# Parameters in the rows of the first input tile, first weights in pieces of two steps, first loads held in order

## The chip, the cores and the metric

The kernel runs on one core of one Trainium2 chip. The metric is the device time of one execution in microseconds; a kernel's time is the median of several runs.

## The reference

The reference is a decoder trunk of two layers on one sequence of 1024 tokens with 1024 features, in float32. Each layer is

```
h = rmsnorm(x, attn_norm);  proj = h @ w_in            # split among four mixers
y = latent attention | gated convolution | causal pooling | sliding-window attention
x = x + (rmsnorm of each group(y) * mix_norm) @ w_o
gate, up = split(rmsnorm(x, ffn_norm) @ w_gate_up);  x = x + (silu(gate) * up) @ w_down
```

and a last rmsnorm follows the layers. The part that matters here is the very first one: the norm of x, and the products of x with the columns of `w_in` that give the keys, the values and the queries of the sliding-window attention.

## The kernel before

Everything is held transposed: features on the 128 partitions, tokens along the rows. The 1024 features are eight *steps* k of 128, the 1024 tokens two *halves* t of 512, so x is sixteen tiles x(t,k) of 128 x 512. A float32 product is made of three products of a faster type: each operand is split into a high half (a rounded copy by ScalarE, L363 or, with a gain, L368) and a low half (the remainder, by VectorE, L366 or L369), and `mm3` (L343) adds high x high, high x low and low x high in PSUM. Each x(t,k) is multiplied by its gain `attn_norm`, a column of the tile `par` that holds all norm weights of the program. The factor 1/rms comes after the product: the squares of x are summed tile by tile (L398, L407, L415, L409), and TensorE adds over the partitions with a matrix of ones (L426).

The opening of layer 0 stands in the order L559 to L617. TensorE runs `WARM` products of ones with ones (L562), while the first loads arrive. The weights of keys and values (`wkv`) are loaded each in two halves of four steps (`first_half`, L472) and split (`first_split`); the tiles of x come through `enter_load` (L458), the parameters in a load of their own (L565), the raw weights of the first queries at L573. Then for each half of the tokens and each step, `enter` splits x(t,k), the key and the value product take it (`first_terms`), and `enter_sum` adds its squares. The query products (`proj`) follow.

SBUF is cut into 47 places of 128 x 1024 numbers (`Slots`), taken as pairs or as halves; a load into a half that was used before must wait until its readers are done. The order of instructions is not the written one: `scheduled_kernel` traces the program, `Order` plans a start for every instruction of each engine from a table of costs and its due times, tries small random shifts (`improve`), and imposes the order found on all engines, SyncE's loads among them. `behind(a, b)` adds a rule without a wait to this: a must stand behind b on its engine. Buffers and PSUM banks are given out from the planned ends too, so an edit at the start can move instructions anywhere.

Of the kernel before, what the change touches and what calls it, by code (L numbers as in the profile page):

```python
# [14 lines left out]
F32 = mybir.dt.float32  # L15
# [5 lines left out]
P = 128  # L21
D = 1024
S = 1024
L = 2
HT = 512
NK = D // P
# [15 lines left out]

NSP = 3
NG = NFF // 2
WARM = 12
DN_SUMS = tuple(range(4, 20))
DN_MADE = ()

# [2 lines left out]
PC_N = 39  # L51
# [74 lines left out]
def trunk_kernel(ctx: ExitStack, tc: tile.TileContext, ins, out, given=None, ends=None):  # L126
# [11 lines left out]
    R, F = View(slots, F32R), View(slots, F32)  # L138
# [2 lines left out]
        return ap.bitcast(F32)  # L141


    par = cpool.tile([P, L * PC_N + NK], F32, name="par")
    cst = cpool.tile([P, CC_N], F32, name="cst")
    ident = cst[:, CC_ID : CC_ID + P]
    ones = cpool.tile([P, P], F32, name="ones")
# [189 lines left out]
    def mm3(o, terms, start=True, stop=True, again=False):  # L337

        nonlocal last_mm
        n = len(terms)  # L340
        for k, (wh, wl, rh, rl) in enumerate(terms):
            for i, (w, r) in enumerate(((wh, rh), (wh, rl), (wl, rh))):
                last_mm = pe.matmul(  # L343
                    o,
                    w,
                    r,
                    start=start and k == 0 and i == 0,
                    stop=stop and k == n - 1 and i == 2,
                    skip_group_check=again,
                )  # L350
# [10 lines left out]
    def split(hi, lo, f, gain=None, after=None):  # L361
        if gain is None:
            a = act.copy(hi, f)  # L363
            if after is not None:
                behind(a, after)
            dve.tensor_tensor(out=lo, in0=f, in1=rd(hi), op=ALU.subtract)  # L366
        else:
            a = act.activation(hi, f, AF.Copy, scale=gain)  # L368
            dve.scalar_tensor_tensor(  # L369
                out=lo, in0=f, scalar=gain, in1=rd(hi), op0=ALU.mult, op1=ALU.subtract  # L370
            )
        return a
# [82 lines left out]

    def enter_load(t, k):
        s = xf[k][t] = F.half()
        sp.dma_start(F.ap(s), x_in[k, :, t * HT : (t + 1) * HT])  # L458

    def enter(t, k):  # L460
        if xf[k][t] is None:
            enter_load(t, k)
        hh[k][t] = half_split(F.ap(xf[k][t]), pcol(0, PC_ATTN + k))
# [2 lines left out]
        ss.add(t, F.ap(xf[k][t]))  # L466
        F.free(xf[k][t])

    def first_half(w, i):

        s = F.half()
        sp.dma_start(F.ap(s), w[2][:, i * HT : (i + 1) * HT])  # L472
        w[3].append(s)

    def first_split(w, i):

        cs = slice(i * HT, (i + 1) * HT)
        split(R.ap2(w[0])[:, cs], R.ap2(w[1])[:, cs], F.ap(w[3][i]))
        F.free(w[3][i])

    def first_terms(w, t, k):
        hi, lo = (R.ap2(i)[:, k * P : (k + 1) * P] for i in w[:2])
        return [(hi, lo, R.ap(hh[k][t][0]), R.ap(hh[k][t][1]))]

    def finish(x, t, cols):
# [15 lines left out]
    for l in range(L):  # L501
# [57 lines left out]
        if l == 0:  # L559
            warm = ps("pv")  # L560
            for i in range(WARM):
                pe.matmul(warm[:, :P], ones, ones, start=True, stop=True)  # L562
            wkv = [(R.pair(), R.pair(), ins["w_in"][0, m], []) for m in (2, 3)]
            enter_load(0, 0)
            sp.dma_start(par, ins["params"])  # L565
            for i in range(2):
                for w in wkv:
                    first_half(w, i)
                for k in range(4 * i, 4 * i + 4):
                    if k:  # L570
                        enter_load(0, k)
            raw = F.pair()
            sp.dma_start(F.ap2(raw), ins["w_in"][0, 0])  # L573
            for k in range(NK):
                enter_load(1, k)
            sp.dma_start(cst, ins["const"])
            pkv = []
            for t in range(2):
                pkv.append([ps("mm"), ps("s")])
                for k in range(NK):  # L580
                    if t == 0 and k % 4 == 0:
                        for w in wkv:
                            first_split(w, k // 4)
                    enter(t, k)
                    for p, w in zip(pkv[t], wkv):
                        mm3(p, first_terms(w, t, k), k == 0, k == NK - 1)
                    enter_sum(t, k)
                if t == 0:
                    wq0 = tuple(R.ap2(i) for i in ring_next())
                    split(*wq0, F.ap2(raw))  # L590
                    F.free_pair(raw)
                    pq = [proj(wq0, 0, "s")]
                ratt[t] = ss.rnorm(t)
            dve.tensor_copy(e_r, cst[:, CC_E : CC_E + P])
            for i in range(L):
                for o, c, n in ((nsink, PC_SINK, 4), (nffn, PC_FFN, NK)):
                    dve.tensor_scalar(
                        out=o[:, i * n : i * n + n],
                        in0=par[:, i * PC_N + c : i * PC_N + c + n],
                        scalar1=-1.0,  # L600
                        scalar2=None,
                        op0=ALU.mult,
                    )
            for v in wkv:
                R.free_pair(v[0])
                R.free_pair(v[1])
            pk, pv_ = zip(*pkv)
            pq.append(proj(wq0, 1, "t"))
        else:
            wk = take()  # L610
            pk = [proj(wk, 0, "s")]
            wv = take()
            pv_ = [proj(wv, 0, "s")]
            pk.append(proj(wk, 1))
            pv_.append(proj(wv, 1, "s"))
            w = take()
            pq = [proj(w, 0, "s"), proj(w, 1, "t")]  # L617
# [1632 lines left out]
def _layout(i):  # L2250
    def tiles(w):

        l, k, n = w.shape
        return w.reshape(l, k // P, P, n // P, P).transpose(0, 3, 2, 1, 4)

    def cols(v):

        return v.reshape(L, -1, P).transpose(2, 0, 1)

    c = np.ascontiguousarray  # L2260
    a = {}
    a["xT"] = c(i["x"].reshape(S, D).T).reshape(NK, P, S)
    w = i["w_in"]
    o = np.cumsum([0, 256, 128, 32, 256, 256, 256, 256, 256, 128, 128])
    cq, ckv, kr, gb, gc, u, pl, q, k, v = (w[:, :, o[n] : o[n + 1]] for n in range(10))
    a["w_in"] = c(
        tiles(
            np.concatenate(
                [q, k, v]
                + [t[:, :, s : s + P] for s in (0, P) for t in (u, gc, gb)]  # L2270
                + [cq, ckv, pl],
                axis=2,
            )
        )
    ).reshape(L, 15, P, D)
    kr = np.concatenate([kr, kr[:, :, 16:], kr[:, :, :16]], axis=2)
    a["w_kr"] = c(kr.reshape(L, NK, P, 64).transpose(0, 2, 1, 3)).reshape(L, P, HT)
    uq = i["w_uq"].reshape(L, 2, P, HEADS, 96)
    uq = np.concatenate([uq, uq[..., 80:], uq[..., 64:80]], axis=4)
    a["w_uq"] = c(uq.transpose(0, 2, 3, 1, 4)).reshape(L, P, 1024)  # L2280
    ukv = i["w_ukv"].reshape(L, P, HEADS, 2, 64)
    a["w_ukv"] = c(ukv.transpose(0, 1, 3, 2, 4)).reshape(L, P, 512)
    a["w_o"] = c(tiles(i["w_o"])).reshape(L, NK, P, D)

    gu = tiles(i["w_gate_up"]).reshape(L, 2, NFF, P, NK // 2, 2, P).transpose(0, 1, 2, 3, 5, 4, 6)

    a["w_gu"] = c(
        np.stack(
            [
                np.stack([gu[:, 0, :, :, 0], gu[:, 1, :, :, 1]], axis=3),  # L2290
                np.stack([gu[:, 0, :, :, 1], gu[:, 1, :, :, 0]], axis=3),
            ],
            axis=2,
        )
    ).reshape(L, NFF, 2, P, D)
    dn = tiles(i["w_down"]).reshape(L, NK // 2, 2, P, NG, 2, P)

    a["w_dn"] = c(dn.transpose(0, 1, 2, 5, 3, 4, 6)).reshape(L, NK // 2, 4, P, NG * P)
    pw = np.zeros((L, P, 2, 2, 64), i["pool_w"].dtype)
    for ct in range(2):  # L2300
        for g in range(2):
            pw[:, 64 * g : 64 * g + 64, ct, g] = i["pool_w"][:, 2 * ct + g]
    a["pool_w"] = c(pw.reshape(L, P, 256))
    conv = i["conv_w"].reshape(L, 3, 2, P).transpose(3, 0, 1, 2).reshape(P, L, 6)
    sinks = np.broadcast_to(i["swa_sinks"][None], (P, L, 4))
    lay = np.concatenate(
        [
            cols(i["attn_norm"]),
            cols(i["ffn_norm"]),
            cols(i["mix_norm"]),  # L2310
            cols(i["mla_q_norm"]),
            cols(i["mla_kv_norm"]),
            conv,
            cols(i["pool_scale"]),
            sinks,
        ],
        axis=2,
    )
    fin = i["final_norm"].reshape(NK, P).T
    a["params"] = c(np.concatenate([lay.reshape(P, -1), fin], axis=1))  # L2320
    a["rope_q"], a["rope_k"], a["const"] = _constants()
    return a

# [27 lines left out]
```

## Time and profile before

| | |
|---|---|
| median of 3 runs | 2038.76 us (2038.35 to 2038.97) |
| the profiled execution | 2038.94 us, of it span 2037.2 us |
| busy TensorE | 2023.3 us (99%) |
| busy VectorE, ScalarE, GpSimd | 1543.7 us (76%), 1015.1 us (50%), 564.1 us (28%) |
| granted TensorE clock | 0.999 |

The span runs from the first instruction to the last; 1.7 us of the execution's time lie around it. Engines are PE (TensorE), DVE (VectorE), ACT (ScalarE), POOL (GpSimd) and SP (SyncE, which issues the loads). A row of the timeline has the start, the duration, the engine, the line of the kernel, the operation and what it writes and reads; behind `[` stands how long the engine was idle before and what ended that. Matmuls overlap, so the pitch from one to the next is what counts, not the duration of one.

### The profile page before, as it was taken

The numbers are of one execution on the slowest core, as the hardware profiler recorded it, in microseconds if no ns is written. First come the engines' busy times: TensorE is split into PE (matmuls) and PEld (weight loads), VectorE is DVE, ScalarE is ACT, GpSimd is POOL, SyncE is SP. The second block draws the span as 40 slices with busy tenths as digits, with TensorE's granted clock in tenths as the row PEclk, the third lists the DMA queues.
The fourth block names the chain that finished last, engine by engine and source line by source line (L and its number), as shares of the span: only waits on it lengthen the run. The fifth ranks groups of instructions, "written<-read, shape, count | busy, mean of one in ns | idle before, by whom it ended". The sixth has DMA issues, their size and how long they took to land.

```text
span 2037.2 us, 26750 instructions
## 1 busy us (share of the span) xinstructions
PE 2023.3 (99%) x9422; PEld 1677.9 (82%) x9422; DVE 1543.7 (76%) x2449; ACT 1015.1 (50%) x1766; POOL 564.1 (28%) x428
## 2 busy tenths in 40 slices
PE   9999999999999999999999999999999999999998
PEld 7887888878888888888888878888888888888887
DVE  8779979997677778767646898889966766775555
ACT  7447657753333335555533676677433333354342
POOL 0100000047776783000001000000677777710000
PEclk9999999999999999999999999999999999999999
DMA  5531222434555556999835223242454555487552
GB/s 206 106 66 47 72 97 82 155 124 166 187 178 188 177 173 238 367 344 325 283 118 122 63 93 120 92 144 96 146 194 170 194 175 169 160 293 266 182 185 84
DMA packets 154231, 338.56 MB, mean 166 GB/s; under 512 B 15088, under 2 KB 62192, under 8 KB 154096
## 3 DMA queue, kind: packets, MB, share of 16 engines
q1 hardware_dynamic: 149616, 325.31, 46.3%
q0 software_dynamic: 4480, 11.54, 3.2%
q8 instruction: 74, 1.21, 0.2%
q14 instruction: 61, 0.50, 0.1%
HBM read 241.36 MB, written 105.91 MB: 170 GB/s over the span
## 4 chain that ended last, share of the span: by engine, by line
PE 97%; DVE 1%; issue 1%; ACT 0%; DMA 0%; POOL 0%; SPq 0%; DVEq 0%; ACTq 0%; POOLq 0%
PE ps_mm L343 38%; PE ps_s L343 29%; PE ps_t L343 12%; PE ps_pv L343 8%; PE ps_pv L1111 2%; PE ps_t L1099 1%; PE ps_s L1045 1%; PE ps_s L1047 1%; PE ps_s L1046 1%; PE ps_s L659 1%; PE ps_s L917 1%; PE ps_pv L720 1%; PE ps_t L708 1%; PE ps_t L423 0%; DVE u L366 0%
## 5 line engine op out<-in xcount | busy, mean ns | idle before, releaser
L343 PE MATMUL ps_mm<-u,u 128*128 128x512 f32 (+1 forms) x3378 | 831.9, 389 | 2.1 <-ACT u L368 0.7
L343 PEld LDWEIGHTS ps_mm<-u,u 128*128 128x128 f32 x3378 | 616.1, 188 | 125.4 <-issue 2.4
L343 PE MATMUL ps_s<-u,u 128*128 128x512 f32 x2670 | 636.4, 390 | 0.7 <-ACT u L1339 0.5
L366 DVE TENSOR_TENSOR u<-u,u 128x1024 fp32r<-128x1024 f32 (+3 forms) x429 | 493.8, 1174 | 187.4 <-ACT u L363 131.1
L363 ACT CAST u<-u 128x1024 fp32r<-128x1024 f32 (+3 forms) x429 | 370.6, 883 | 443.4 <-PE ps_mm L343 62.8
L343 PEld LDWEIGHTS ps_s<-u,u 128*128 128x128 f32 x2670 | 500.9, 188 | 107.0 <-ACT u L1339 1.3
L343 PE MATMUL ps_t<-u,u 128*128 128x512 f32 (+1 forms) x1124 | 256.3, 378 | 0.1
L343 PEld LDWEIGHTS ps_t<-u,u 128*128 128x128 f32 x1124 | 202.5, 188 | 40.8 <-DVE u L1515 1.5
L1523 POOL TENSOR_TENSOR tp<-tp,u 128x512 f32<-128x512 f32 x80 | 125.0, 1562 | 352.3 <-ACT tp L1521 215.9
L343 PE MATMUL ps_pv<-u,u 128*128 128x512 f32 x744 | 177.1, 389 | 0.0
L343 PEld LDWEIGHTS ps_pv<-u,u 128*128 128x128 f32 x744 | 139.7, 188 | 29.0
L317 POOL DMA_DIRECT2D gd<-in_w_gu x24 | 21.4, 894 | 415.8 <-PE ps_t L343 282.0
L1108 POOL MEMSET u<- 128x128 f32 x32 | 6.3, 223 | 427.4 <-PE ps_pv L1111 117.6
L1521 ACT ACTIVATE tp<-tp 128x512 f32<-128x512 f32 x80 | 50.6, 633 | 129.3 <-DVE tp L442 129.2
L363 ACT CAST u<-ps_t 128x512 fp32r<-128x512 f32 (+3 forms) x132 | 64.7, 503 | 55.4 <-PE ps_t L1099 29.1
L366 DVE TENSOR_TENSOR u<-ps_t,u 128x512 fp32r<-128x512 f32 (+3 forms) x132 | 74.7, 580 | 13.3 <-ACT u L363 12.4
L368 ACT ACTIVATE u<-u,par 128x512 fp32r<-128x512 f32 x100 | 70.2, 717 | 29.2 <-DVE u L442 9.1
L1601 POOL TENSOR_TENSOR u<-u 128x352 f32<-128x352 f32 x64 | 77.0, 1204 | 8.6 <-DMA u<-in_w_dn 8.1
L369 DVE SCALAR_TENSOR_TENSOR u<-u,par,u 128x512 fp32r<-128x512 f32 x100 | 73.2, 746 | 6.3 <-ACT u L368 6.2
L1311 POOL TENSOR_TENSOR u<-u 128x512 f32<-128x512 f32 x38 | 69.9, 1840 | 27.2 <-DVE u L366 25.3
L1601 POOL TENSOR_TENSOR u<-u,u 128x352 f32<-128x352 f32 x64 | 76.4, 1194 | 2.7
L442 DVE TENSOR_TENSOR tp<-tp,u 128x512 f32<-128x512 f32 x76 | 75.3, 990 | 2.0
(204 smaller groups left out, 2314.0 us busy)
## 6 DMA issues: line engine op xcount, KB each, us to landing
u<-in_w_gu SPq DMA_DIRECT2D x84, 512.0 KB, 4.0
ad<-u SPq DMA_DIRECT2D x154, 256.0 KB, 2.4
u<-ad SPq DMA_DIRECT2D x70, 512.0 KB, 5.8
u<-in_w_dn SPq DMA_DIRECT2D x64, 352.0 KB, 3.4
qd<-u SPq DMA_DIRECT2D x64, 352.0 KB, 3.5
u<-in_w_in SPq DMA_DIRECT2D x43, 512.0 KB, 5.3
u<-qd SPq DMA_DIRECT2D x32, 512.0 KB, 5.5
u<-in_w_dn SPq DMA_DIRECT2D x24, 512.0 KB, 5.4
```

The source lines that it names most:

```text
L317: paced(pool.dma_start(d, a, **more))
L343: last_mm = pe.matmul(o, w, r, start=start and k == 0 and i == 0, stop=stop and k == n - 1 and i == 2, skip_group_check=again,)
L363: a = act.copy(hi, f)
L366: dve.tensor_tensor(out=lo, in0=f, in1=rd(hi), op=ALU.subtract)
L368: a = act.activation(hi, f, AF.Copy, scale=gain)
L369: dve.scalar_tensor_tensor(out=lo, in0=f, scalar=gain, in1=rd(hi), op0=ALU.mult, op1=ALU.subtract)
L442: dve.tensor_tensor(out=o, in0=a, in1=b, op=ALU.mult)
L1111: pe.matmul(py[:, c0:], v_of(j, h), R.ap(s)[:, c0:], start=j == 0 and n == 0, stop=j == nj - 1 and n == 1,)
L1311: pool.tensor_tensor(out=q4, in0=q4, in1=F.ap(self.raw[1] + 1), op=ALU.add)
L1521: last_silu = act.activation(g, g, AF.Silu)
L1523: pool.tensor_tensor(out=g, in0=g, in1=r, op=ALU.mult)
L1601: pool.tensor_tensor(out=o, in0=a, in1=b, op=ALU.add)
```

## The change

The parameters have no load of their own any more: they stand behind the numbers of x(0,0) in the rows of one array, `first`, of 128 x 598, which lands in a pair of halves; the gain of x(0,0) is read there, VectorE copies the parameters from the pair's second half to `par`, and this half becomes free. The first weights come in four pieces of two steps each, a piece of 512 columns holding both products (`w_first`). The loads of pieces and of the first half's tiles are tied to each other in the written order by `behind`. The warm-up has ten products in place of twelve.

```diff
-WARM = 12
+WARM = 10
...
     def enter_load(t, k):
         s = xf[k][t] = F.half()
-        sp.dma_start(F.ap(s), x_in[k, :, t * HT : (t + 1) * HT])
+        return sp.dma_start(F.ap(s), x_in[k, :, t * HT : (t + 1) * HT])
+
+    def enter_first():
+        s = F.pair()
+        loads.append(sp.dma_start(F.ap2(s)[:, : HT + PC_ALL], ins["first"]))
+        xf[0][0] = s
+        got = F.ap(s + 1)[:, :PC_ALL]
+        hh[0][0] = half_split(F.ap(s), got[:, PC_ATTN : PC_ATTN + 1])
+        dve.tensor_copy(par, got)
+        F.free(s + 1)
...
-    def first_half(w, i):
-        s = F.half()
-        sp.dma_start(F.ap(s), w[2][:, i * HT : (i + 1) * HT])
-        w[3].append(s)
-    def first_split(w, i):
-        cs = slice(i * HT, (i + 1) * HT)
-        split(R.ap2(w[0])[:, cs], R.ap2(w[1])[:, cs], F.ap(w[3][i]))
-        F.free(w[3][i])
-    def first_terms(w, t, k):
-        hi, lo = (R.ap2(i)[:, k * P : (k + 1) * P] for i in w[:2])
+    def first_terms(i, t, k):
+        cs = slice(2 * i * P + k % 2 * P, 2 * i * P + k % 2 * P + P)
+        hi, lo = (R.ap(v)[:, cs] for v in wkv[k // 2])
         return [(hi, lo, R.ap(hh[k][t][0]), R.ap(hh[k][t][1]))]
...
-            wkv = [(R.pair(), R.pair(), ins["w_in"][0, m], []) for m in (2, 3)]
-            enter_load(0, 0)
-            sp.dma_start(par, ins["params"])
-            for i in range(2):
-                for w in wkv:
-                    first_half(w, i)
-                for k in range(4 * i, 4 * i + 4):
-                    if k:
-                        enter_load(0, k)
+            wkv, wraw, loads = [], [], []
+            for j in range(NK // 2):
+                wraw.append(F.half())
+                loads.append(sp.dma_start(F.ap(wraw[j]), ins["w_first"][j]))
+                if j == 0:
+                    wkv.append(half_split(F.ap(wraw[0])))
+                    F.free(wraw[0])
+                    enter_first()
+                else:
+                    loads.append(enter_load(0, 2 * j))
+                loads.append(enter_load(0, 2 * j + 1))
+            for a, b in zip(loads[1:], loads):
+                behind(a, b)
             raw = F.pair()
             sp.dma_start(F.ap2(raw), ins["w_in"][0, 0])
...
-                    if t == 0 and k % 4 == 0:
-                        for w in wkv:
-                            first_split(w, k // 4)
-                    enter(t, k)
-                    for p, w in zip(pkv[t], wkv):
-                        mm3(p, first_terms(w, t, k), k == 0, k == NK - 1)
+                    if t == 0 and k and k % 2 == 0:
+                        wkv.append(half_split(F.ap(wraw[k // 2])))
+                        F.free(wraw[k // 2])
+                    if t or k:
+                        enter(t, k)
+                    for i, p in enumerate(pkv[t]):
+                        mm3(p, first_terms(i, t, k), k == 0, k == NK - 1)
```

SyncE's first loads before: `u4` to `u9` hold pieces of the weights of keys and values (L472) and the tiles x(0,0) to x(0,7) (L458), `par` the parameters, `u10` the raw query weights, `u11` and what follows the tiles of the second half.

```order
L472 DMA u4_120<-in_w_in 128x512
L458 DMA u4_120<-in_xT 128x512
L565 DMA par_75<-in_params 128x86
L472 DMA u5_124<-in_w_in 128x512
L458 DMA u5_124<-in_xT 128x512
L458 DMA u6_127<-in_xT 128x512 x2
L472 DMA u7_130<-in_w_in 128x512
L458 DMA u8_133<-in_xT 128x512
L472 DMA u7_130<-in_w_in 128x512
L458 DMA u8_133<-in_xT 128x512
L458 DMA u9_136<-in_xT 128x512 x2
L573 DMA u10_139<-in_w_in 128x1024
```

SyncE's first loads of the changed kernel: `u0` is the first piece of weights, `u2` the new first transfer; `u9` the raw query weights; the eight loads to `u8`, `u10`, `u11`, `u12` and `u13` are the tiles x(1,k) of the second half; the next load to `u2` is x(0,1), and `u4` takes the second piece of weights.

```order
L567 DMA u0_114<-in_w_first 128x512
L465 DMA u2_119<-in_first 128x598
L578 DMA u9_140<-in_w_in 128x1024
L459 DMA u8_138<-in_xT 128x512
L459 DMA u10_143<-in_xT 128x512
L459 DMA u11_146<-in_xT 128x512
L459 DMA u12_149<-in_xT 128x512
L459 DMA u13_152<-in_xT 128x512
L459 DMA u10_143<-in_xT 128x512
L459 DMA u11_146<-in_xT 128x512
L459 DMA u12_149<-in_xT 128x512
L459 DMA u2_119<-in_xT 128x512
```

x(0,1), which stood fifth, now stands twelfth, behind the query weights and all of the second half.

TensorE before, from the second real product on: `u15` is x(0,0), `u16` x(0,1), `u17` x(0,2), high and low half each; `u0` to `u3` are the weights of keys (`ps_mm`) and values (`ps_s`).

```order
L343 MATMUL ps_s_155<-u15_160,u2_118 128x512 x2
L343 MATMUL ps_mm_154<-u16_170,u0_116 128x512
L343 MATMUL ps_s_155<-u15_160,u3_119 128x512
L343 MATMUL ps_s_155<-u16_170,u2_118 128x512
L343 MATMUL ps_mm_154<-u16_170,u0_116 128x512
L343 MATMUL ps_mm_154<-u16_170,u1_117 128x512
L343 MATMUL ps_s_155<-u16_170,u2_118 128x512
L343 MATMUL ps_s_155<-u16_170,u3_119 128x512
L343 MATMUL ps_mm_154<-u17_182,u0_116 128x512
```

TensorE of the changed kernel, from the last product of x(0,0) with the first piece `u1` on: `u3` is x(0,0), `u24` and `u25` the high and low half of the query weights (`ps_s_261`), `u26` is x(1,0), `u27` x(1,1) and `u14` x(0,1); `ps_mm_295` and `ps_s_296` are the keys and values of the second half.

```order
L344 MATMUL ps_mm_155<-u3_121,u1_116 128x512
L344 MATMUL ps_s_261<-u3_121,u24_257 128x512 x2
L344 MATMUL ps_mm_295<-u26_297,u1_116 128x512
L344 MATMUL ps_s_296<-u26_297,u1_116 128x512
L344 MATMUL ps_s_261<-u3_121,u25_258 128x512
L344 MATMUL ps_mm_295<-u26_297,u1_116 128x512
L344 MATMUL ps_s_296<-u26_297,u1_116 128x512 x2
L344 MATMUL ps_s_296<-u27_307,u1_116 128x512 x3
L344 MATMUL ps_mm_295<-u26_297,u1_116 128x512
L344 MATMUL ps_mm_295<-u27_307,u1_116 128x512 x3
L344 MATMUL ps_s_156<-u14_164,u1_116 128x512
```

After x(0,0), TensorE now takes 3 products of the queries and 12 of the second half with the steps 0 and 1, and only then x(0,1).

More of the change, by code (lines that the diff above doesn't have):

```diff
@@ L141, in rd @@
         return ap.bitcast(F32)
-    par = cpool.tile([P, L * PC_N + NK], F32, name="par")
+    PC_ALL = L * PC_N + NK
+    par = cpool.tile([P, PC_ALL], F32, name="par")
     cst = cpool.tile([P, CC_N], F32, name="cst")
@@ L604, in trunk_kernel @@
             for v in wkv:
-                R.free_pair(v[0])
-                R.free_pair(v[1])
+                R.free(v[0])
+                R.free(v[1])
             pk, pv_ = zip(*pkv)
@@ L2319, in _layout @@
     fin = i["final_norm"].reshape(NK, P).T
-    a["params"] = c(np.concatenate([lay.reshape(P, -1), fin], axis=1))
+    a["first"] = c(np.concatenate([a["xT"][0, :, :HT], lay.reshape(P, -1), fin], axis=1))
+    two = a["w_in"][0, 2:4].reshape(2, P, NK // 2, 2 * P)
+    a["w_first"] = c(two.transpose(2, 1, 0, 3)).reshape(NK // 2, P, HT)
     a["rope_q"], a["rope_k"], a["const"] = _constants()
```

## The prediction

> **What bounds the kernel now.** I read the page's busy shares and chain first, then the stretches of the whole program, then the first 43 us in the timeline and the chain of waits.
>
> ```profile
> span 2037.2 us, 26750 instructions
> PE 2023.3 (99%) x9422; PEld 1677.9 (82%) x9422; DVE 1543.7 (76%) x2449; ACT 1015.1 (50%) x1766; POOL 564.1 (28%) x428
> PE 97%; DVE 1%; issue 1%; ACT 0%; DMA 0%; POOL 0%; SPq 0%; DVEq 0%; ACTq 0%; POOLq 0%
> ```
>
> TensorE ends almost everything: 97% of the chain is its own work. So a change can only move the time by moving TensorE's idle time, and the stretches show where that lies.
>
> ```profile
> core 0: us, PE busy (x) PEld busy (x) DVE busy (x) ACT busy (x) POOL busy (x), PEclk, DMA share, GB/s
> 0.00:42.60 42.60, 41.33 (x174) 32.99 (x175) 35.81 (x58) 34.48 (x56) 0.20 (x4) 1.00 0.60 216
> 42.60:430.00 387.40, 385.66 (x1890) 318.12 (x1888) 339.15 (x749) 241.96 (x522) 19.86 (x31) 1.00 0.31 89
> 430.00:1000.00 570.00, 569.95 (x2512) 471.08 (x2511) 420.98 (x438) 249.41 (x329) 260.85 (x181) 1.00 0.67 235
> 1000.00:1350.00 350.00, 349.07 (x1742) 291.26 (x1742) 263.37 (x640) 201.84 (x455) 13.84 (x28) 1.00 0.37 109
> 1350.00:2000.00 650.00, 649.73 (x2892) 537.85 (x2891) 464.73 (x526) 281.90 (x394) 269.37 (x184) 1.00 0.53 182
> ```
>
> From 42.6 to 2000 us TensorE is idle 1.74 + 0.05 + 0.93 + 0.27 = 2.99 us, out of 1957. The change rewrites the stretch before 42.6 us, where the first keys, values and queries are made:
>
> ```profile
> 0.75 0.39 SPq L472 DMA_DIRECT2D u<-in_w_in  x1
> 1.06 5.49 PE L562 MATMUL ps_pv<-ones 128*128 128x128 f32 x24 [1.06 <-DVE ones L148]
> 1.20 0.42 SPq L458 DMA_DIRECT2D u<-in_xT  x1
> 1.67 0.42 SPq L565 DMA_DIRECT2D par<-in_params  x1
> 3.49 0.62 ACT L363 CAST u<-u 128x512 fp32r<-128x512 f32 x1 [1.47 <-DMA u<-in_w_in]
> 5.94 0.72 ACT L368 ACTIVATE u<-u,par 128x512 fp32r<-128x512 f32 x1 [1.83 <-DMA par<-in_params]
> 6.71 1.52 PE L343 MATMUL ps_mm<-u,u 128*128 128x512 f32 x3 [0.16 <-ACT u L368]
> ```
>
> The warm-up products (12, each shown as two rows) end at 1.06 + 5.49 = 6.55; ScalarE gets the parameters only at 5.9, and the first real product starts at 6.71. The chain says what that costs:
>
> ```profile
> 1.67 4.18 DMA par<-in_params
> 20.58 0.86 PE ps_t L426 x2
> 35.98 0.93 PE ps_t L426 x2
> 37.15 5.46 PE ps_t L343 x24
> ```
>
> One real product takes 5.46 / 24 = 0.2275 us. The opening has 144 of them (keys and values 2 x 2 x 24, queries 2 x 24) and two norm sums of 0.86 and 0.93: 144 x 0.2275 + 1.79 = 34.55 us of work. It ends at 37.15 + 5.46 = 42.61, that is 36.06 after the warm-up: 1.5 us are lost to waits.
>
> **The change, part by part.** *Warm-up.* Two products fewer are four rows of 5.49 / 24 = 0.229 us: the warm-up ends at 1.06 + 20 x 0.229 = 5.64, which is 0.92 earlier. Nothing hides this, if data are there.
>
> *Parameters.* Their own load is gone, and with it ScalarE's 1.83 us of waiting. What is late next comes from the order of loads, whose rate these rows give:
>
> ```profile
> u<-in_w_in SPq DMA_DIRECT2D x1, 256.0 KB, 2.7
> u<-in_xT SPq DMA_DIRECT2D x1, 256.0 KB, 2.9
> par<-in_params SPq DMA_DIRECT2D x1, 43.0 KB, 4.2
> u<-in_w_in SPq DMA_DIRECT2D x1, 256.0 KB, 4.8
> 2.13 0.43 SPq L472 DMA_DIRECT2D u<-in_w_in  x1
> 10.00:20.00 10.00, 10.00 (x45) 7.99 (x44) 9.90 (x16) 10.00 (x18) 0.00 (x0) 1.00 1.06 403
> ```
>
> The first two land at 0.75 + 2.7 = 3.45 and 1.20 + 2.9 = 4.1, 0.65 apart, in the order issued. The parameters, six times smaller, land at 1.67 + 4.2 = 5.87, and the next weights at 2.13 + 4.8 = 6.9. From 10 us on the rate is 403 GB/s, 0.65 us for 256 KB; I take 0.66. The new first transfer (128 x 598, 299 KB) then lands at 3.45 + 0.78 = 4.25. The operations on it cost:
>
> ```profile
> L368 ACT ACTIVATE u<-u,par x16: 704/709/725, 5.9 to 24.8; 128x512 fp32r<-128x512 f32 x16
> L369 DVE SCALAR_TENSOR_TENSOR u<-u,par,u x16: 745/749/752, 6.7 to 26.5; 128x512 fp32r<-128x512 f32 x16
> 16.29 1.04 ACT L363 CAST u<-u 128x1024 fp32r<-128x1024 f32 x1
> 18.23 1.22 DVE L366 TENSOR_TENSOR u<-u,u 128x1024 fp32r<-128x1024 f32 x1
> 19.51 1.93 ACT L368 ACTIVATE u<-u,par 128x512 fp32r<-128x512 f32 x3
> 19.96 4.06 DVE L369 SCALAR_TENSOR_TENSOR u<-u,par,u 128x512 fp32r<-128x512 f32 x6
> 23.94 0.22 DVE L594 CAST e_r<-cst 128x128 fp32r<-128x128 f32 x1
> ```
>
> ScalarE has the high half at 4.3 + 0.71 = 5.0. VectorE's new copy of the parameters (nearest row: 0.22 for 128x128) lies after the low half of the weights, which ends about 4.8, so the low half of x ends at 5.0 + 0.75 = 5.8. TensorE starts at 5.64 and needs that half for its third product only: nothing delays the start, 1.07 us earlier than 6.71, and the copy costs nothing.
>
> *Order of loads.* This gives it back. The second tile of the first half of the tokens, x(0,1), is loaded into the free half of the first tile's buffer, so SyncE must wait until the parameters have been copied out of it, and every later load of this chain is held behind it. What is not in the chain overtakes it in the built order: the raw query weights and all eight tiles of the second half. x(0,1) then lands at 4.25 + 1.30 (512 KB) + 8 x 0.66 + 0.66 = 11.5. That every other load was in time there hides nothing, because TensorE runs out: ahead of x(0,1) stand 6 products of x(0,0), 3 of the queries and 12 of x(1,0) and x(1,1), 21 in all. From 5.64 they end at 5.64 + 21 x 0.2275 = 10.4. One wait lies within them: the low half of x(1,0) follows that of the query weights on VectorE. These land at 5.55; ScalarE ends them at 5.55 + 1.04 = 6.6, VectorE at 6.65 + 1.22 = 7.9 and x(1,0) at 8.55, where TensorE would be at 8.1: 0.4 more, 10.85. ScalarE has the high half of x(0,1) at 11.55 + 0.71 = 12.25. TensorE waits 1.4 us (should its slow clock of the start, below, last beyond 5.64, the first products take longer and this wait shrinks by as much), and 144 - 21 = 123 products follow: 12.3 + 123 x 0.2275 + 1.79 = 42.1. To this I add 0.75 for VectorE: a pair of steps is two low halves (pitch 4.06 / 6 = 0.68), two sums of about that and one low half of weights, 3.3 us, against 12 key and value products of 2.7, with queries put between; where a low half is just late, two or three waits of 0.25. End 42.8: **0.2 us later** than 42.6.
>
> The unknown is the rate at the start. From 4.1 to 6.9 us the trace lands 43 + 256 KB, which at 403 GB/s take 0.74: 2.0 us are lost. If the parameters' short rows (86 numbers, 344 bytes) did it, the figures above hold; if it is a property of the start, the same 2.0 us fall on the new loads, x(0,1) lands at 13.5 and the end is 44.8, **2.2 later**. A gain at this place is excluded, since the first two landings and the full rate leave none. I take +0.5, near the low end, because the slow stretch begins with these rows. [...]
>
> *The splits* of the first weights are as many as before (four of 512 columns, L363 and L366), two steps for both products in place of four for one; they cost the same.
>
> *The rest.* The schedule of the whole program is worked out anew: TensorE's order also differs up to about 430 us and in the second layer's attention. The work is the same. What the new waits are no row can show. At most the 2.99 us of later idleness are gained; a loss I bound by its doubling, +3, since almost all of it already lies in the stretches that are reordered. I take 0.
>
> Sum, against the profiled execution: span 2037.2, its own time 2038.94, so 1.74 lies around the span; 2038.94 + 0.5 = 2039.4. The median of the runs shown is 0.18 below the profiled execution, so the forecast for the median is 2038.76 + 0.5 = **2039.3**.
>
> **The rivals.** *The clock drops in the wait.* The trace shows this at the end:
>
> ```profile
> 2027.44 0.70 PE L430 MATMUL ps_s<-tn,ones 128*128 128x256 f32 x2 [0.59 <-ACT tn L429]
> 2031.00:2032.00 1.00, 0.00 (x0) 0.00 (x0) 1.00 (x3) 0.00 (x0) 0.00 (x0) 0.68 0.00 0
> 20.41 1.02 PE L426 MATMUL ps_t<-u,ones 128*128 128x512 f32 x2
> ```
>
> TensorE ends at 2028.14, and a granted clock of 0.68 over 2031 to 2032 is half speed from 2031.36: 3.2 us of idleness do it. The warm-up rows take 0.229 us for 128 columns, while four times the columns take 0.51 (L426): the first 6 us ran at half speed, though the stretch from 0 to 42.6 shows 1.00. With loads at the slow end TensorE is idle from 10.85 to 13.55 + 0.71 = 14.25, 3.4 us, just over that. Then some 6 us run at half speed and lose 3: 2.2 + 3 on 2038.76 is **2044.0**, slower. Against it: at full rate the wait is 1.4 us. The decisive point is x(0,1) landing after about 13.3. [...]
>
> *The new schedule is worse or better later.* Worse by 3: 2042.3, still within my bound; worse by 4 or more, slower at 2043. Better by all of the 2.99: 2036.3. For a change speaks that the reordered places are those with the idle time; against large moves, that the long stretches from 430 to 1000 and from 1350 on have almost none.
>
> *The early start stays.* If VectorE and the loads keep up, without a wait at x(0,1), the opening keeps the 0.92 of the warm-up and loses 1.0 to waits in place of 1.5: 1.4 earlier, **2037.4**. The landing times speak against it.
>
> **How the numbers follow.** 0.2%, 4.1 us, is about what a measurement of this kernel can tell from no change. Forecast (opening +0.2 to +2.2, rest within 2) 0.64; clock drop 0.06, slower; later schedule worse 0.14, of it 0.05 by over 4.1; better 0.06, of it 0.04 by over 4.1 together with an early start; early start alone 0.10. Slower 0.06 + 0.05 = 0.11; faster 0.04; within 0.85. The range leaves out the two slower cases and the large gain, 0.15: 2036.0 (all later idle gone) to 2043.0 (+2.2 in the opening and 2.0 later).
>
> **What would show it.** Right: warm-up over at 5.6, first real product then, an idle TensorE of about 1.4 us near 11 ended by ScalarE's L369 on x(0,1), the last query product over near 42.8, and about 3 us of idleness from there to 2000. Wrong: no wait near 11 (early start), a granted clock of 0.5 behind it (clock), or a time off by over 4 us whose idle lies after 43 us (schedule).

## The result, and the profile after

| | before | changed |
|---|---|---|
| median | 2038.74 us (2037.87 to 2039.17, 22 runs) | 2041.51 us (2040.35 to 2043.51, 22 runs) |
| profiled execution | 2038.94 us, span 2037.2 | 2042.29 us, span 2040.5 |

The changed kernel takes 1.0014 times as long, with a 95% interval of 1.0009 to 1.002: 2.8 us more. That is less than the 4.1 us that the prediction called no change, and within its range, but the interval lies above 1. The forecast was 2039.3. The single runs also spread more: 3.2 us against 1.3.

The page of the changed kernel, its span, busy times and chain:

```profile
span 2040.5 us, 26752 instructions
PE 2023.9 (99%) x9418; PEld 1677.3 (82%) x9418; DVE 1548.1 (76%) x2450; ACT 1013.5 (50%) x1766; POOL 562.1 (28%) x428
PE 91%; DVE 5%; ACT 1%; issue 1%; DMA 1%; POOL 0%; SPq 0%; DVEq 0%; POOLq 0%; ACTq 0%
```

Its stretches, cut at the same times (TensorE's busy time is the second number behind the colon):

```profile
0.00:42.60 42.60, 37.48 (x149) 29.30 (x150) 32.82 (x55) 31.49 (x50) 0.20 (x4) 0.96 0.61 216
42.60:430.00 387.40, 386.22 (x1896) 318.71 (x1894) 339.77 (x748) 242.40 (x522) 16.76 (x30) 1.00 0.29 87
430.00:1000.00 570.00, 569.94 (x2513) 471.26 (x2514) 421.25 (x438) 248.69 (x328) 264.57 (x182) 1.00 0.67 234
1000.00:1350.00 350.00, 349.65 (x1741) 291.72 (x1739) 264.15 (x639) 201.37 (x454) 13.45 (x28) 1.00 0.38 111
1350.00:2000.00 650.00, 649.52 (x2879) 536.16 (x2878) 469.43 (x528) 281.98 (x395) 267.08 (x184) 1.00 0.53 183
```

The loss is in the first row: TensorE is busy 37.48 us there in place of 41.33, and the granted clock, 1.00 before, is 0.96. Behind 42.6 us TensorE is idle 1.18 + 0.06 + 0.35 + 0.48 = 2.07 us, less than the 2.99 of before. The timeline of TensorE in the opening, rows picked:

```profile
1.06 4.63 PE L563 MATMUL ps_pv<-ones 128*128 128x128 f32 x20 [1.06 <-DVE ones L149]
5.84 0.51 PE L344 MATMUL ps_mm<-u,u 128*128 128x512 f32 x1
...
8.88 0.73 PE L344 MATMUL ps_s<-u,u 128*128 128x512 f32 x2 [1.39 <-ACT u L364]
9.98 0.50 PE L344 MATMUL ps_mm<-u,u 128*128 128x512 f32 x1 [0.37 <-ACT u L369]
...
12.31 1.08 PE L344 MATMUL ps_mm<-u,u 128*128 128x512 f32 x4
15.54 0.50 PE L344 MATMUL ps_s<-u,u 128*128 128x512 f32 x1 [2.15 <-ACT u L369]
```

The warm-up is over at 5.69 and the first product starts at 5.84, 0.87 earlier than before. Then come three waits: 1.39 us for ScalarE's high half of the query weights, 0.37 for that of a tile of the second half, 2.15 for that of x(0,1). Its load stands in the chain:

```profile
2.60 7.46 DMA u<-in_xT
10.09 5.41 ACT u L369 x8
...
42.72 4.58 PE ps_t L344 x20
```

The last query product, and with it the opening, ends at 42.72 + 4.58 = 47.30, where it ended at 42.61: 4.7 us later. Three loads by their rows in the DMA view (the first tile issued at 1.20, the query weights at 1.66, x(0,1) at 9.20; the last number is the time to landing):

```profile
u<-in_first SPq DMA_DIRECT2D x1, 299.0 KB, 2.9
u<-in_w_in SPq DMA_DIRECT2D x1, 512.0 KB, 6.1
u<-in_xT SPq DMA_DIRECT2D x1, 256.0 KB, 5.5
```

The first tile lands at 4.1, the query weights at 7.76 and x(0,1) at 14.7. The granted clock is 0.50 from 16.17 to 19.59 and is followed here in stretches of that length, 3.41 us, counted back from the fall. The stretch that holds the last wait is followed by one at half the clock, the one that holds the first wait (first row) is not:

```profile
5.93:9.34 3.41, 2.02 (x8) 1.27 (x8) 0.48 (x1) 1.18 (x2) 0.00 (x0) 1.00 0.93 311
...
12.76:16.17 3.41, 1.26 (x6) 0.73 (x5) 2.85 (x5) 3.41 (x7) 0.00 (x0) 1.00 1.02 363
16.17:19.59 3.42, 3.42 (x10) 2.64 (x9) 3.42 (x7) 3.42 (x7) 0.00 (x0) 0.50 1.06 370
19.59:23.00 3.41, 3.41 (x17) 2.80 (x16) 3.41 (x6) 3.41 (x7) 0.00 (x0) 1.00 1.00 411
```

Ten products in the stretch at half the clock against seventeen in the next: by the granted 0.50, half of 3.42, 1.71 us, is lost to the clock.

### The profile page after: what moved, and what is told of

Read it like the earlier page. It is cut to its first block, busy times and chain, and to the rows that moved or that the text cites. A ratio compares the mean times of both kernels' runs of the same rounds, so it can differ in the third digit from the quotient of the medians.

```text
span 2040.5 us, 26752 instructions
## 1 busy us (share of the span) xinstructions
PE 2023.9 (99%) x9418; PEld 1677.3 (82%) x9418; DVE 1548.1 (76%) x2450; ACT 1013.5 (50%) x1766; POOL 562.1 (28%) x428
## 4 chain that ended last, share of the span: by engine, by line
PE 91%; DVE 5%; ACT 1%; issue 1%; DMA 1%; POOL 0%; SPq 0%; DVEq 0%; POOLq 0%; ACTq 0%
PE ps_mm L344 36%; PE ps_s L344 28%; PE ps_t L344 11%; PE ps_pv L344 8%; PE ps_pv L1117 2%; PE ps_t L1105 2%; DVE u L367 1%; PE ps_s L1051 1%; PE ps_s L1053 1%; PE ps_s L1052 1%; PE ps_s L665 1%; PE ps_s L923 1%; PE ps_pv L726 1%; PE ps_t L714 1%; DVE u L416 1%
## 5 line engine op out<-in xcount | busy, mean ns | idle before, releaser
L1529 POOL TENSOR_TENSOR tp<-tp,u 128x512 f32<-128x512 f32 x80 | 119.5, 1494 | 342.8 <-ACT tp L1527 342.8
L369 ACT ACTIVATE u<-u,par 128x512 fp32r<-128x512 f32 x99 | 69.5, 718 | 26.9 <-DVE u L443 8.8
```

Source lines behind the costliest of these rows:

```text
L1529: pool.tensor_tensor(out=g, in0=g, in1=r, op=ALU.mult)
```

## The experiments

For every profiled execution below two numbers say where its time lies against before's: by how much later the TensorE instruction with the same number, counted from the end of the program, starts near 160 us ("opening"; the order of instructions can differ), and what is added from there to the end ("rest"). Their sum is the difference of the spans. For the changed kernel they are +4.7 and -1.4. A second execution of it shows how far one profile can be trusted.

**The changed kernel again** (no edit).

> The changed kernel once more, for a second profile of the opening. If the clock fell in the first profile because most of one of its windows was idle, it need not fall here: without it the opening ends 1 to 2 earlier than 47.3, with x(0,1) landing anywhere from 12 to 15. If it falls again after the wait for x(0,1), the fall belongs to the wait.

One run, 2042.55 us, span 2040.8: opening +3.8, rest -0.2. So about 1 us in either number is from execution to execution. x(0,1) lands at 13.8, TensorE waits 2.30, and the clock falls again, for one stretch, behind a stretch with 1.11 us of work:

```profile
11.80:15.21 3.41, 1.11 (x6) 0.59 (x5) 2.81 (x5) 3.41 (x7) 0.00 (x0) 1.00 1.06 390
15.21:18.63 3.42, 3.42 (x10) 2.64 (x9) 3.42 (x7) 3.42 (x7) 0.00 (x0) 0.50 1.06 392
```

**A buffer of its own for x(0,1).** The half with the parameters is given back only when all first loads have their places, so SyncE doesn't have to wait for the copy.

```diff
-        F.free(s + 1)
+        return s + 1
...
-                    enter_first()
+                    spare = enter_first()
...
+            F.free(spare)
             for a, b in zip(loads[1:], loads):
```

> The changed kernel, except that the half behind x(0,0), which brings the parameters, is given free only after all first loads are written, so x(0,1) has a buffer of its own and the built order of loads is the written one (x(0,1) third, query weights after all of the first half). Theory 'late tile': the loss comes from x(0,1) landing at 14.7 us behind nine other loads; here it lands before 7, no wait of TensorE over 1 us stands between 5.8 and 20, the clock does not fall there, the last query product of the opening is over by 42 (47.3 in the changed kernel), and the time is 2036 to 2038.5. Rival 'short warm-up': ten warm-up products leave the clock low or TensorE waiting anyway; the time stays over 2040. Rival 'new schedule': the loss lies after 43 us and comes with any new schedule; the opening ends near 42 but the time stays over 2040.

2037.77 us against 2038.57: 0.9995 (0.9986 to 1.0004). Opening -1.2, rest -0.1. x(0,1) is issued third, at 1.67, and lands at 5.87. DMA row, timeline and chain:

```profile
u<-in_xT SPq DMA_DIRECT2D x1, 256.0 KB, 4.2
```

```profile
5.82 0.47 PE L344 MATMUL ps_mm<-u,u 128*128 128x512 f32 x1
...
8.90 0.39 PE L344 MATMUL ps_s<-u,u 128*128 128x512 f32 x1
9.39 0.96 PE L344 MATMUL ps_mm<-u,u 128*128 128x512 f32 x3
```

```profile
35.95 5.45 PE ps_t L344 x24
```

Behind the start and up to 45 us no wait of 0.15 us or more is shown, the granted clock is 1.00 over the first 160 us, and the opening ends at 41.40, 1.2 before the 42.61 of before. All other parts of the change are in this kernel; the one edit takes the loss away.

**The same lateness without the shared buffer.** From the kernel above: its own buffer stays, but x(0,1) is put behind the query weights and the eight tiles of the second half by rule.

```diff
                     spare = enter_first()
+                    raw = F.pair()
+                    loads.append(sp.dma_start(F.ap2(raw), ins["w_in"][0, 0]))
+                    for k in range(NK):
+                        loads.append(enter_load(1, k))
```

> The kernel with a buffer of its own for x(0,1), but with its load put by the held order where the changed kernel has it: behind the query weights and all eight tiles of the second half. Theory 'late tile': the place in the order is all that counts, not the shared buffer: x(0,1) lands between 11.5 and 15, TensorE waits 1 us or more for it, the opening ends 2 to 5 later than before (44.5 to 47.5) and the time is 2041 within 1.2. Rival 'shared buffer': the wait for the copy out of the shared half did it; without it the opening ends near 42 and the time stays under 2039.

2043.08 us against 2038.94: 1.0019 (1.001 to 1.0027), 2 us over the expected 2041. Opening +1.9, rest +1.5, in the fastest of the eleven executions. x(0,1) is issued at 7.79 and lands at 13.2; TensorE waits for it, here too, by 0.81 us, behind waits of 0.60 and 0.53 for the two halves of the query weights:

```profile
u<-in_xT SPq DMA_DIRECT2D x1, 256.0 KB, 5.4
```

```profile
12.63 0.61 PE L344 MATMUL ps_s<-u,u 128*128 128x512 f32 x2
14.05 0.50 PE L344 MATMUL ps_mm<-u,u 128*128 128x512 f32 x1 [0.81 <-ACT u L369]
```

```profile
40.37 4.12 PE ps_t L344 x18
```

The opening ends at 44.49, at the lower edge of what was expected. So the place in the order of loads is enough to make the opening late, and the shared half only brings it about. The clock doesn't fall in this execution (1.00 over the first 160 us). The +1.5 behind the opening isn't explained by it.

**Other schedules of the same work.** The numbers that `improve` draws are changed, in each of the three kernels.

```diff
-        draw = random.Random(1)
+        draw = random.Random(2)
```

> The kernel before with another start of the random numbers that the planner uses for its small shifts; the work, the loads and the written order are the same. Rival 'new schedule': a new draw alone moves the time by 2 us or more. Theory 'late tile': it moves it by less than 1 (2037.7 to 2039.7), so the 2.8 us of the change are not explained by a new draw.

> The kernel with a buffer of its own for x(0,1), with another start of the planner's random numbers. If its gain is made in the opening, that ends near 41.6 again (about 1 earlier than before) and the time is 2037.8 within 1; if its 0.8 was luck of the schedule, the opening is the same and the time moves by more than 1, or goes back to 2038.6.

> The changed kernel with another start of the planner's random numbers; the loads stand in the same order, x(0,1) twelfth. Theory 'late tile': the opening again ends 2 to 5 later than before, and the time is 2041.5 within 1.2. Rival 'new schedule': the 2.8 us came with one unlucky schedule, and this one is back under 2040.

Before with other numbers: 1.0003 (0.9994 to 1.0012), opening -0.3, rest +0.9. The own buffer: 2037.30 us, 0.9992 (0.9983 to 1.0), opening -1.6, rest +0.4. The changed kernel: 2043.01 us, 1.0019 (1.0011 to 1.0028), opening +1.9, rest +0.1 in a profiled execution that was 2 us below its median; the time is 0.3 over what was expected, the opening just under. So with both draws the opening is late where x(0,1) is, and early where it is early. The last one has a wait of 1.99 us for x(0,1) and no fall of the clock (1.00 over the first 160 us); as cut here, its idle time is spread over two stretches:

```profile
9.33:12.74 3.41, 2.75 (x12) 1.80 (x10) 3.41 (x7) 3.41 (x6) 0.00 (x0) 1.00 1.05 395
12.74:16.15 3.41, 2.08 (x9) 1.74 (x10) 2.82 (x6) 3.41 (x6) 0.00 (x0) 1.00 1.05 386
```

**The warm-up.** Twelve products in the changed kernel, ten in the one before, eight in the one with its own buffer.

```diff
-WARM = 10
+WARM = 12
```

> The changed kernel with twelve warm-up products in place of ten. Theory 'late tile': the first real product starts at 6.7 in place of 5.8, TensorE waits 0.9 less for x(0,1), which lands at the same 14 to 15 us; the time is that of the changed kernel, 2041.5 within 1, perhaps up to 1 less where the shorter wait keeps the clock. Rival 'short warm-up': the time goes back to that of the kernel before, 2038.7 within 0.7.

```diff
-WARM = 12
+WARM = 10
```

> The kernel before with ten warm-up products in place of twelve, nothing else. Theory 'late tile': the parameters land at 5.85 as before, so the first real product stays near 6.7 and the time within 0.5 of 2038.7. Rival 'short warm-up': the gap of 1 us before the first product, or a later rise of the clock, costs 1.5 or more: 2040.2 and up.

```diff
-WARM = 10
+WARM = 8
```

> The kernel with a buffer of its own for x(0,1), with eight warm-up products in place of ten. The warm-up ends near 4.7, ScalarE has x(0,0) at 5.0, so the first product starts 0.7 earlier, near 5.1. Theory 'late tile': TensorE then waits for loads near 6 to 9 and gains at most 0.4 in the opening; time 2037.5 within 1. Rival 'short warm-up': the clock rises later or falls again, the opening ends 1 or more later than with ten (41.6), time over 2038.8.

The changed kernel with twelve stays slow: 2042.42 us, 1.0017 (1.0008 to 1.0026); opening +1.7 without a fall of the clock (1.00 over the first 160 us), rest +0.7. So the shorter warm-up didn't cost the time. Its first product starts at 5.75 all the same, not at the expected 6.7 (the start is taken up below). Before with ten is slower, 2040.79 us, 1.001 (1.0001 to 1.0019): the expectation of 2038.7 within 0.5 failed, and the time is one that the rival 'short warm-up' gave. But the loss isn't where a short warm-up would act: the opening is -0.1, the rest +2.0. The first product starts at 5.84 here too, as the parameters landed at 4.82 and not at 5.85, and the loss is in the long stretches. Of 500 to 800 us, before and then this kernel:

```profile
500.00:800.00 300.00, 299.95 (x1322) 247.50 (x1321) 216.26 (x210) 107.71 (x147) 210.66 (x149) 1.00 0.53 180
```

```profile
500.00:800.00 300.00, 299.87 (x1317) 245.72 (x1316) 210.97 (x210) 106.37 (x145) 213.68 (x149) 1.00 0.54 179
```

Five products fewer in the same time (1.1 us at 0.2275), with almost no idle time shown; what slows them the rows don't say, and it stays open. With eight, 2039.29 us, 1.0003 (0.9994 to 1.0011): opening +0.2, rest +1.4. This too is over what was expected and in the rival's range, but the last query product is over at 41.49, as early as with ten (41.40). Between there and 160 us TensorE is idle for 0.88 us, all of it from 80 to 100 us. A gain from a still shorter warm-up isn't shown.

**The parts alone.** Only the parameters in the first tile's rows (with a buffer of its own for x(0,1), and the weights as before), then only the pieces and the order, with the parameters in their own load and twelve warm-up products.

```diff
-            enter_load(0, 0)
-            sp.dma_start(par, ins["params"])
+            spare = enter_first()
...
+            F.free(spare)
             raw = F.pair()
```

> The kernel before with one part of the change: the parameters in the rows of x(0,0). Their half is given free after the first loads, the weights stay in halves of four steps, no loads are held, twelve warm-up products. Theory 'late tile': no part of the change costs much by itself, only x(0,1) put last; here it lands before 8, the warm-up (to 6.55) or the second piece of weights sets the first products, the opening ends within 1 of 42.6, and the time is 2038.6 within 1.2. Rival: the packed row or the copy by VectorE costs by itself, the opening ends 2 or more later and the time is over 2040.5 with that loss before 43 us.

```diff
-WARM = 10
+WARM = 12
...
-                    enter_first()
+                    loads.append(enter_load(0, 0))
+                    loads.append(sp.dma_start(par, ins["params"]))
```

> The kernel before with the other part: first weights in pieces of two steps and the first loads held in the written order, the parameters in a load of their own behind x(0,0), twelve warm-up products. Theory 'late tile': x(0,1) is fourth in the order and lands before 8; the opening ends within 1 of 42.6, the time is 2038.6 within 1.2. Rival: pieces or held loads cost by themselves, the opening ends 2 or more later.

The first: 2040.31 us, 1.0008 (0.9999 to 1.0017), opening +0.6, rest +1.4: the opening is as expected, the time 0.5 over. It has a wait of its own on a tile that lands 2.3 us behind the load ahead of it:

```profile
10.44 0.51 PE L344 MATMUL ps_mm<-u,u 128*128 128x512 f32 x1 [1.21 <-ACT u L369]
```

The second: 2039.75 us, 1.0003 (0.9994 to 1.0012), opening +0.1, rest +2.4, in the slowest of its eleven executions, 1.75 us over their median. Neither part makes the loss of the opening by itself.

**Without the held order.** From the changed kernel the rule between the first loads is taken away.

```diff
-            for a, b in zip(loads[1:], loads):
-                behind(a, b)
```

> The changed kernel without the rule that holds the first loads in the written order. The built order then has the query weights second, three pieces of weights before or beside them, the first piece only seventh and x(0,1) eleventh or later. Theory 'late tile': the first products wait for the first piece (landing near 8 to 9) and x(0,1) is as late as before, so the opening ends 3 to 6 later than before; time 2041 to 2045. Rival 'held order': the rule itself is what costs; without it the time is under 2040.

2043.50 us, 1.002 (1.0011 to 1.0029), opening +4.5, rest -0.2. Now a piece of the weights is late, and TensorE waits within its first products:

```profile
6.75 2.05 PE L344 MATMUL ps_s<-u,u 128*128 128x512 f32 x3 [1.05 <-ACT u L364]
10.54 0.79 PE L344 MATMUL ps_s<-u,u 128*128 128x512 f32 x1 [1.74 <-ACT u L364]
```

The waits are only part of this loss. Up to 13.58 the products follow each other at about 0.43 us, from there on at 0.23: 7 of them in one stretch, 16 in the next, though the clock column (the number behind POOL's count) shows 1.00 in both:

```profile
10.17:13.58 3.41, 3.04 (x7) 2.04 (x8) 2.97 (x5) 3.35 (x6) 0.00 (x0) 1.00 1.05 396
13.58:17.00 3.42, 3.42 (x16) 2.73 (x17) 3.42 (x6) 3.42 (x7) 0.00 (x0) 1.00 1.05 386
```

So TensorE's first ten products ran at the pitch that the changed kernel shows at a granted 0.50: 0.43, from 16.90 to 17.33. The first of them starts at 6.75, about where before's did (6.71), and the last query product is over 3.9 later; the second wait is 1.74 of that, which leaves about 2 us for the slow pitch, an estimate from these rows. Taking the rule away puts nothing right: the planner's order starves TensorE in another place, so the rule isn't what has to go.

Taken together: the five kernels with a load that TensorE needs early put behind others (changed, with other numbers, with twelve, late by rule, without the rule) have openings of +1.7 to +4.7 and ratios of 1.0014 to 1.002 with intervals above 1; the other seven have openings of -1.6 to +0.6. One of the seven, before with ten warm-up products, has an interval above 1 too, with its loss behind the opening. The kernel with its own buffer is the best version: its two schedules are 0.8 and 1.45 us below before, yet each interval reaches 1, so that it beats before is likely, not shown. That it beats the changed kernel is: its intervals end at 1.0004 and 1.0, the changed kernel's starts at 1.0009.

## Why the prediction was right or wrong

*Start and copy: right, the size of the gain by luck.* The warm-up was forecast to end at 5.64 and ended at 5.69, with the first product at 5.84; the copy of the parameters is this row of VectorE, over well before that product:

```profile
4.59 0.20 DVE L469 COPY par<-u 128x86 f32<-128x86 f32 x1
```

But the 6.55 of before, from which the gain of 0.92 was counted, belongs to one execution. The five profiles with twelve products end the warm-up between 5.44 and 6.55, those with ten between 5.41 and 5.70. In before nine of the 24 rows are over at 3.35 and all at 6.55: fifteen in 3.20 us, 0.213 each to the end. In before with other numbers the same 24 rows, which took 5.49 us, take 4.38 (in the changed kernel with twelve 4.54). If the last of them came at half the pitch, that began at about 4.1, an estimate from these times:

```profile
1.06 4.38 PE L562 MATMUL ps_pv<-ones 128*128 128x128 f32 x24 [1.06 <-DVE ones L148]
```

*The mechanism: right in the main.* The wait that gives back the early start was placed at x(0,1), ended by ScalarE's L369. The trace has it there, the own buffer removes it and the late load restores it. But it isn't the first wait: 1.39 us for the query weights and 0.37 for x(1,0) stand ahead of it, where the prediction had 0.4 in all, and these alone give back more than the 0.87 by which TensorE started earlier.

*The landing of x(0,1): the step that failed.* The prediction took 11.5, with 13.5 as the upper bound; it is 14.7 and 13.8 in the changed kernel and 12.6 to 13.3 in its relatives. The 512 KB behind the first tile were to take 1.30 us and took 7.76 - 4.08 = 3.68 (1.8 to 3.0 in the four other profiles with this order: the second one of the changed kernel, other numbers, twelve, late by rule). The first two tiles of the second half, landing at 9.12 and 10.06, were 1.0 later still than 0.66 each. The choice of the low end rested on a reason, that the slow stretch begins with the short rows of the parameters. The runs show that such rows aren't needed for it: the changed kernel has no such load, and its slow stretch is as bad. In slices of 0.4 us from the start, the rates in GB/s of before, and then of the changed kernel:

```profile
GB/s 0 0 0 0 56 302 348 388 259 144 217 235 271 261 282 266 210 215 353 369 374 364 369 374 389 374 399 410 415 430 410 410 430 379 405 399 394 364 399 405
```

```profile
GB/s 0 0 0 0 102 179 391 360 385 311 184 287 179 215 184 189 246 277 312 307 353 379 394 410 405 410 405 405 410 374 348 358 379 353 369 399 399 348 343 338
```

Both come near 350 or more about 2.5 us after the program's start, fall to 144 to 312 until about 7 or 8 us, and go up to 400 only then. The kernel with its own buffer dips less, to 225 to 338. The loads that land between 4 and 8 us pass through the dip; which one comes late differs from kernel to kernel. What makes the dip was not tried and stays open.

*What followed from it.* The 21 products ahead of x(0,1) ended at 12.31 + 1.08 = 13.39 in place of 10.85, since the query weights were late too, and TensorE went on at 15.54 in place of 12.25: 3.3 us. The clock took 1.7. The 0.75 added for VectorE were too much by about 0.5: from 15.54 to 47.30 are 31.76 us, less 1.71 for the clock and 29.77 of work leaves 0.28. 3.3 + 1.7 - 0.5 = 4.5, the difference between 47.30 and the forecast 42.8.

*The clock rival: too small a chance.* It had 0.06, its condition being a landing after 13.3 and 3.2 us without a product. Both profiles of the changed kernel show the fall, after landings at 14.7 and 13.8 but with only 2.15 and 2.30 us of idleness. What fits these runs is the idle share of one stretch of 3.41 us: 2.15 of 3.41 (63%) and 2.30 (67%) were followed by half the clock, 1.33 (39%) and 0.66, from a wait of 1.99, were not, nor was the 1.39 (41%) of the changed kernel's first wait. But the border that splits the 1.99 lies where the stretches were cut, at 12.74; no trace shows one there. A limit on a single wait, between 1.99 and 2.15 us, would fit these numbers as well, though the clock fell only at 16.17 and 15.21, some 0.6 us after the products had come back at 15.54 and 14.61. Which of the two holds isn't shown, nor that the clock goes by windows at all, as the expectation for the second execution supposed. The price was 1.7, half of the 3.42 us at 0.50, and not the 3 that the prediction took from the slow 6 us of the start.

*The rest at nothing: right within its bounds.* -1.4 and -0.2 in the two profiles of the changed kernel, -0.2 to +2.4 in all others. The bound of 3 held; but kernels that merely differ in the schedule lie mostly above before, by about 1 us on the mean of the eleven. So the total of one rebuilt kernel can mislead by as much as the effect looked for, and only the place of the loss tells.

*The early start* as a rival was given 2037.4, if no wait came; the kernel with its own buffer, where none comes, has 2037.77, 0.8 under before where the rival had 1.4. *The total* came out as no change by the prediction's bound, and +0.5 was too little by 2.3. That it lies within the range is luck in part: the opening was bounded by +2.2 and lost 4.7 and 3.8 in the two profiles, which fits in only because the range left 2 us for the rest, and the rest of the first profile happened to give back 1.4.

## What to carry to other kernels

When a load is put into space that an early reader must first give up, look at what overtakes it in the queue: a wait of some 3 us for the copy (from 1.67 to 4.79) became a place nine loads further back. When two explanations of a slow stretch fit the trace of one kernel, keep both prices in the forecast; the convenient one was wrong. After an edit that redraws the whole schedule, judge by the stage in which the time moved, since the total also carries 1 to 2 us of luck from the stages that the edit didn't touch. And a gain counted from one profile needs a second one: the start of 6.55 was the latest of five.

## What was not expected of the hardware

The granted clock of TensorE fell to 0.50 after a stretch of 3.41 us in which TensorE was still busy for 1.26 us in the changed kernel and 1.11 in its second execution, and came back after 3.42 us, at 19.59 and 18.63. A wait of 2.15 us thus cost 1.7 more, and one of 1.99 (the changed kernel with other numbers) was followed by no fall, which fits the wider spread of the changed kernel's runs, 3.2 us against 1.3 (that the clock causes the spread was not tested). At the start the slow pitch of TensorE lasted to anywhere between about 4.1 us (before with other numbers, the estimate above) and 13.58 (without the rule, 0.43 us a product against 0.23 behind it), while the clock column showed 1.00. The rate of the first loads dips between 4 and 8 us, from 350 and more to 144 to 312 GB/s, in before with its short rows and in the changed kernel without them.
